# Two pads that move the weight tiles of a hybrid decoder layer to another place within 256 bytes

## The chip, the cores and the metric

The kernel runs on one core of one Trainium2 chip. The metric is the device time of one execution, in microseconds (us); the median of three runs is taken. Engines are named as in the profile: PE (the matrix engine, its matmuls), PEld (its loads of stationary weights, which overlap matmuls), DVE (vector), ACT (scalar), POOL and SP.

## The reference

One layer on 512 tokens of 1024 channels, in float32. Three sub-layers, each with an RMS norm, a scale and shift that come from a conditioning vector, and a gate on the residual:

```
h = modulate(rmsnorm(x, g1), sh1, sc1);  x = x + 0.5 * gt1 * ((silu(h @ w1_gate) * (h @ w1_up)) @ w1_down)
h = modulate(rmsnorm(x, gm), sh2, sc2);  x = x + gt2 * hybrid_mixer(h)
h = modulate(rmsnorm(x, g2), sh3, sc3);  x = x + 0.5 * gt3 * ((silu(h @ w2_gate) * (h @ w2_up)) @ w2_down)
return rmsnorm(x, g_final)
```

The SwiGLU width is 2816. The mixer has one input projection, a gated convolution of width 3 on 512 channels, attention of 8 heads with a compressed and two full branches, group norms and an output projection. Of all this the two SwiGLU layers and the two projections of the mixer are most of the arithmetic.

## The kernel before

**Products.** Every large product is made of three matmuls, to keep float32 precision: each operand is split into a high and a low part of type fp32r, and `mm3` (L280) issues high by high, high weights by the low part of the moving operand, and low weights by the high part. A matmul loads a stationary block of 128x128 (the weights: tiles `whi`, `wlo`) and streams a moving operand of 512 or 256 columns (the activations: `hhi`, `hlo` for the normed residual, `ghi`, `glo` for the gated hidden values). All of them come from line L278, so the profile tells them apart by tile names: `b<-hhi,whi` writes a PSUM bank from moving `hhi` and weights `whi`.

**Phases.** SwiGLU one, mixer, SwiGLU two. A phase begins with `first_products` or `first_group` (L576): six column blocks grow side by side, channel block by channel block, as the parts of h come. In the mixer and in SwiGLU two these are halves of 256 tokens. Then whole column blocks follow with 512 columns (`project` L545, `part` L609). The last two channel blocks of a SwiGLU (`main`, last loop) are again made in halves of 256 tokens.

**Weights.** Units of up to 1024 columns come from HBM into four tiles `raw` (L326), ACT copies the high part into one of four tiles `whi` (L366), DVE or POOL subtracts to get the low part in `wlo` (L355). A unit of 1024 columns holds eight blocks of 128 columns, 512 bytes apart in a partition. Some units at the end of a phase are needed twice and have memory of their own: in SwiGLU one two pairs `whik`, `wlok` (L585) from the phase's own pool, in the mixer two tiles `PT`.

**Order.** A list scheduler inside the kernel (`Plan`) gives each engine its instructions once, when the program is built. It knows costs of operations and nothing of addresses.

**Memory.** Tiles of the pool `const` lie one behind the other in each partition. Where a tile begins, in bytes and as the remainder by 256, follows from the sizes of those ahead of it. In this kernel:

| tiles | first begins at | remainder by 256 |
|---|---|---|
| raw0 to raw3 | 53184 | 192 |
| whi0 to whi3, then wlo0 to wlo3 | 69568 | 192 |
| hhi0 to hhi7, hlo0 to hlo7 | 102784 | 128 |
| ghi, glo (SwiGLU one, SwiGLU two) | 160128, 147840 | 128 |
| whik0, wlok0, whik1, wlok1 (SwiGLU one) | 209280 | 128 |
| V (values of the attention, stationary) | 139648 | 128 |
| PT0 to PT3, PT4 (turned probabilities) | 176896, 222368 | 0, 160 |

All sizes involved are multiples of 256, and so are the offsets of the blocks of 128 columns and of the halves of 256 tokens; the remainder holds for every block in these tiles.

Of the kernel before, what the change touches and what calls it, by code (L numbers as in the profile page):

```python
# [10 lines left out]
F32 = mybir.dt.float32  # L11
F32R = mybir.dt.float32r
# [7 lines left out]
P = 128  # L20
T = 512
D = 1024
DK = D // P
F = 2816
FK = F // P
FH = FK // 2
NB = T // P
HD = 64
# [12 lines left out]
# columns of the packed per-channel vectors  # L41
# [8 lines left out]
# columns of the packed constants  # L50
# [9 lines left out]
# slots of memory in turns  # L60
# [27 lines left out]
# the steps to a power of -0.5: (u + RS_P) u + RS_Q is next to u ** -0.5 / c for u about 1, and RS_K = 1 / (4 c c)  # L88
RS_P, RS_Q, RS_K = -3.333049194662436, 4.993328488220333, 1 / (4 * 0.3759002861170453 ** 2)
BATCHES = ((0,), (1,), (2, 3))  # L90
# ranks of the tasks: the lower goes first
# [33 lines left out]
class Slots:  # L125
    """Tokens for memory that is used over and over."""
# [4 lines left out]
    def spare(self, n):  # L131
        """A token, if n more stay idle."""
        return self, n


class Plan:
    """A list schedule of the core's work. Each task is a generator that asks for an engine and a time (or for
    one of several), for an event or for a token, and emits its instructions as the engine falls to it. The engines
    then run what they were given in that order."""

    # from engine (row) to engine (column)
# [105 lines left out]
def c_dma(n):  # L247
    """n: bytes of a partition."""
    return DMA, max(0.05, n * 0.356e-3)
# [6 lines left out]
def tile_hymba_layer(ctx: ExitStack, tc: tile.TileContext, xT, pos, cols_d, con_d, wa0, wa1, f1a, f1b, f1d,  # L256
# [23 lines left out]
    def mm3(o, w, x_, start, stop):  # L280
        """Both operands as (high, low) parts; low times low is below float32's last place."""
        mm(o, w[0], x_[0], start, False)
        mm(o, w[0], x_[1], False, False)
        mm(o, w[1], x_[0], False, stop)

# [41 lines left out]
    whi_of = [const.tile([P, UNIT], F32R, name=f"whi{i}") for i in range(N_W)]  # L327
    wlo_of = [const.tile([P, UNIT], F32R, name=f"wlo{i}") for i in range(N_W)]
# [4 lines left out]
    # the last units of a phase, needed twice, have memory of their own  # L333
# [50 lines left out]
    def rsqrt(v, y, u, alone=False):  # L384
        """y = (v / RS_K) ** -0.5 for normal v > 0: a guess from the exponent, a step of third order, one of second.
        alone: the vector engine takes nothing else in between."""
        guess = float(0x5f3759df - (2 << 23) - (1 << 31))
        yield SMALL
        nc.vector.tensor_scalar(y.bitcast(I32), v.bitcast(I32), -0.5, guess, op0=OP.mult, op1=OP.add)
        if alone:  # L390
            plan.limit[DVE] = R_NORM
        yield SMALL
        nc.vector.scalar_tensor_tensor(u, y, 16.0, y, op0=OP.mult, op1=OP.mult)  # L393
        yield SMALL
        nc.vector.tensor_mul(u, u, v)
        yield SMALL
        nc.vector.scalar_tensor_tensor(u, u, RS_P, u, op0=OP.add, op1=OP.mult)
        yield SMALL
        nc.vector.scalar_tensor_tensor(y, u, RS_Q, y, op0=OP.add, op1=OP.mult)
        yield SMALL  # L400
        nc.vector.scalar_tensor_tensor(u, y, 4.0 / RS_K, y, op0=OP.mult, op1=OP.mult)
        yield SMALL
        nc.vector.tensor_mul(u, u, v)
        yield SMALL
        nc.vector.scalar_tensor_tensor(y, u, 3.0, y, op0=OP.subtract, op1=OP.mult)
        if alone:
            plan.limit[DVE] = 1000

# [10 lines left out]
    class Norm:  # L419
        """1 / rms per token, from the channel blocks as they are ready: on every partition, or for the halves in  # L420
        columns with a token per partition."""
# [7 lines left out]
        def sums(self, i, o, s, start, stop):  # L429
            """Over the partitions of s, tokens on the partitions of the result."""  # L430
            ts = HALVES[i]
            nb = T // 2 // P
            for t in range(nb):
                mm(o[:, t:t + 1], s[:, ts.start + t * P:ts.start + (t + 1) * P], kv("one"), start and t == 0,
                   stop and t == nb - 1)
# [77 lines left out]
    def build_h(s, d, ts, rb, ready, used=lambda: None):  # L513
        """h, in parts: the normed residual, scaled and shifted."""
        n = ts.stop - ts.start
        q = yield scr
        t = scr_of[q][:, :n]
        yield c_stt(n)
        nc.vector.scalar_tensor_tensor(t, x[d][:, ts], am[:, s, d:d + 1], rb(), op0=OP.mult, op1=OP.mult)  # L519
        used()  # L520
        sh = mod[:, 3 * s, d:d + 1]
        yield c_act(n)
        nc.scalar.activation(hhi[d][:, ts], t, AF.Identity, bias=sh)  # L523
        yield c_stt(n)
        nc.vector.scalar_tensor_tensor(hlo[d][:, ts], t, sh, hhi[d][:, ts].bitcast(F32), op0=OP.add, op1=OP.subtract)  # L525
        give(scr, q)
        done(ready)
# [8 lines left out]
    def project(b):  # L536
        """A column block of the products with h, into bank b."""
# [7 lines left out]
    def start_builds(s, norm):  # L545
        """The parts of the next phase's h, as the norm allows."""
# [14 lines left out]
    def first_group(order, built, accs, end, n_cols=2 * GRP):  # L561
        """Some column blocks' products, channel block by channel block, as the parts of h come."""
# [150 lines left out]
    def ada_first(d):  # L713
        """Channel block d's shift and scale: summed over the blocks of c, then over the partitions."""
# [43 lines left out]
    def ada_first_pe(d):  # L758
        """The same by the tensor engine alone, four blocks of c side by side."""
# [51 lines left out]
    def warm():  # L811
        """Keeps the tensor engine at its full clock until the first products."""
# [57 lines left out]
    def ada_reduce(m, j):  # L870
        """Sums over the partitions: four rows of 256 channels, then turned to a channel per partition."""
# [30 lines left out]
    def rope_tables():  # L902
        """cos and sin of position x frequency, in steps; the angle is first taken to [-pi, pi]."""
# [58 lines left out]
    with ExitStack() as mixer:  # L962
# [52 lines left out]
        def rope(b, then, pool, scale=1.0):  # L1015
            """r * cos + swapped r * sin, then then(...). The queries are scaled, and negated: the scores' maxima are
            then the products' minima, as the exponents need them."""
# [51 lines left out]
        def keys(b):  # L1069
            """Per group: the high parts twice, for the queries' two parts; the low parts in place."""  # L1070
# [9 lines left out]
        def query(c):  # L1080
            """Per head: its high parts on the group's partitions, its low parts on the others."""
# [11 lines left out]
        def blocks(src, pn, i):  # L1093
            """The overlapping blocks of a compressed branch, with their position terms, in parts."""
# [40 lines left out]
        def compressed_keys(bs):  # L1135
            """From the two compressions' hidden sums (values, then keys) to their rows."""
# [57 lines left out]
        def compressed(c):  # L1194
            """Gated probabilities of the compressed branch of pair c: [2 x 32 keys, tokens]."""
# [36 lines left out]
            # rows without a valid key are all in the first block of tokens  # L1232
# [20 lines left out]
        # a pair's products with the values' low parts  # L1253
# [4 lines left out]
        def group_norm(y, gcol, n):  # L1258
            """y [P, T], two groups of 64 channels: normed in place."""
# [45 lines left out]
        def scores(c, b, s, n_, order):  # L1305
            """Probabilities of a head and branch, gated; then turned, in parts, for the products with the values."""
# [110 lines left out]
        def values(c, s):  # L1417
            """A head's sums over both branches, low parts of the values on the second 64 partitions."""
# [112 lines left out]
        def receive(f, b, pool, n):  # L1531
            """Starts what follows column block f of the input projection."""
# [150 lines left out]
        def keep():  # L1683
            """The turned probabilities' memory, for units once the attention is over."""
# [18 lines left out]
    with tc.tile_pool(name="g2", bufs=1) as gp:  # L1703
# [33 lines left out]
        def turn(g):  # L1737
            """Four channel blocks by 128 tokens."""
# [31 lines left out]
def _ffn_layout(wg, wu, wd):  # L1770
    g = wg.reshape(DK, P, FK, P)
    u = wu.reshape(DK, P, FK, P)
    gu = np.stack([g, u], axis=3)                      # k, p, f, 2, n
    first = gu[:, :, :GRP].reshape(DK, P, GRP * 2 * P)
    rest = gu[:, :, GRP:].transpose(2, 3, 1, 0, 4).reshape(FK - GRP, 2, P, DK * P)
    dn = wd.reshape(2, FH, P, DK, P)                   # half, k, p, d, n
# [5 lines left out]
def _layout(i):  # L1782
# [10 lines left out]
    def pose(p):  # L1793
        q = p.reshape(16, 2, HD).transpose(2, 1, 0).reshape(HD, 32)   # d, (parity, step)
        return np.concatenate([q, q])
# [41 lines left out]
    first = wa.reshape(DK, P, 9, DK, P)[:, :, :2]      # k, p, (shift, scale), d, n  # L1837
# [23 lines left out]
    wo = np.concatenate([wo[:512], wo[512:][perm]], axis=0).reshape(DK, P, DK, P)   # k, p, d, n  # L1861
# [31 lines left out]
```

## Time and profile before

| | |
|---|---|
| runs | 1083.23, 1082.0, 1084.75 us; median 1083.23 us |
| profiled execution, span from first to last instruction | 1081.2 us |
| what lies around the span, against the median | 2.0 us |
| PE busy | 1062.0 us, 98% |
| PEld busy | 860.6 us, 80% |
| DVE, ACT, POOL busy | 606.7, 409.9, 49.8 us |

The profile lists no time of the profiled execution beside its span, so the second and third line together stand for it. Matmuls are pipelined: the duration that a row gives one matmul overlaps the next one, so what a matmul costs the engine is read from start to start. A row `300.06 0.40 PE ...` of the view in order of time says when it began and how long it is shown; only the first number is used here.

### The profile page before, as it was taken

The numbers are of one execution on the slowest core, as the hardware profiler recorded it, in microseconds if no ns is written. First come the engines' busy times: TensorE is split into PE (matmuls) and PEld (weight loads), VectorE is DVE, ScalarE is ACT, GpSimd is POOL, SyncE is SP. The second block draws the span as 40 slices with busy tenths as digits, with TensorE's granted clock in tenths as the row PEclk, the third lists the DMA queues.
The fourth block names the chain that finished last, engine by engine and source line by source line (L and its number), as shares of the span: only waits on it lengthen the run. The fifth ranks groups of instructions, "written<-read, shape, count | busy, mean of one in ns | idle before, by whom it ended". The sixth has DMA issues, their size and how long they took to land.

```text
span 1081.2 us, 13889 instructions
## 1 busy us (share of the span) xinstructions
PE 1062.0 (98%) x5417; PEld 860.6 (80%) x5417; DVE 606.7 (56%) x1069; ACT 409.9 (38%) x713; POOL 49.8 (5%) x47
## 2 busy tenths in 40 slices
PE   8999999999999999999999999999999999999997
PEld 5777677788888889987777777998888888888887
DVE  4978888833333347499787786654333323333334
ACT  4552222212222233358756785334222122222321
POOL 0310000000000001012001010100000000000000
PEclk8999999999999999999999999999999999999998
DMA  9659989532222230443300003224333333322302
GB/s 333 243 191 326 315 322 327 176 96 85 92 98 98 98 103 16 131 125 122 127 25 28 13 14 96 92 83 132 94 89 91 98 98 98 94 86 93 98 20 78
DMA packets 40706, 133.60 MB, mean 124 GB/s; under 512 B 4704, under 2 KB 8032, under 8 KB 40000
## 3 DMA queue, kind: packets, MB, share of 16 engines
q1 hardware_dynamic: 40640, 132.71, 37.3%
q8 instruction: 42, 0.69, 0.3%
q14 instruction: 24, 0.20, 0.1%
HBM read 130.14 MB, written 2.10 MB: 122 GB/s over the span
## 4 chain that ended last, share of the span: by engine, by line
PE 88%; DVE 5%; DMA 4%; issue 1%; ACT 0%; SPq 0%; DVEq 0%; ACTq 0%
PE b L278 86%; DMA araw<-in_wa_dram 3%; PE b L1396 2%; DVE ada L865 1%; DVE afirst L736 1%; DVE wlo L355 1%; DMA x<-in_xT_dram 1%; DVE s L519 1%; DMA raw<-in_f1b_dram 0%; PE b L1291 0%; DVE afirst L733 0%; DVE v L393 0%; PE b L1241 0%; DVE afirst L728 0%; ACT hhi L523 0%
## 5 line engine op out<-in xcount | busy, mean ns | idle before, releaser
L278 PE MATMUL b<-hhi,whi 128*128 128x512 f32 (+1 forms) x1020 | 386.1, 379 | 0.0
L278 PE MATMUL b<-hlo,whi 128*128 128x512 f32 (+1 forms) x1020 | 379.0, 372 | 0.5 <-DVE hlo L525 0.4
L278 PE MATMUL b<-hhi,wlo 128*128 128x512 f32 (+1 forms) x1020 | 378.7, 371 | 0.0
L366 ACT ACTIVATE whi<-raw 128x1024 fp32r<-128x1024 f32 (+3 forms) x176 | 178.1, 1013 | 461.8 <-PE b L278 319.8
L355 DVE TENSOR_TENSOR wlo<-raw,whi 128x1024 fp32r<-128x1024 f32 (+3 forms) x162 | 191.2, 1180 | 218.4 <-ACT whi L366 213.0
L278 PEld LDWEIGHTS b<-hhi,whi 128*128 128x128 f32 x1020 | 192.3, 189 | 41.5 <-issue 6.7
L278 PEld LDWEIGHTS b<-hhi,wlo 128*128 128x128 f32 x1020 | 192.5, 189 | 36.6
L278 PEld LDWEIGHTS b<-hlo,whi 128*128 128x128 f32 x1020 | 192.7, 189 | 34.9 <-DVE hlo L525 1.2
L278 PE MATMUL b<-ghi,whi 128*128 128x512 f32 (+1 forms) x364 | 138.2, 380 | 0.0
L278 PE MATMUL b<-ghi,wlo 128*128 128x512 f32 (+1 forms) x364 | 137.4, 378 | 0.0
L278 PE MATMUL b<-glo,whi 128*128 128x512 f32 (+1 forms) x364 | 137.4, 378 | 0.0
L600 DVE TENSOR_TENSOR s<-sg,b 128x512 f32<-128x512 f32 x44 | 30.1, 686 | 106.6 <-PE b L278 105.8
L278 PEld LDWEIGHTS b<-ghi,whi 128*128 128x128 f32 x364 | 68.4, 188 | 14.7 <-issue 0.8
L278 PEld LDWEIGHTS b<-ghi,wlo 128*128 128x128 f32 x364 | 68.5, 188 | 14.0
L278 PEld LDWEIGHTS b<-glo,whi 128*128 128x128 f32 x364 | 68.5, 188 | 13.9
L865 DVE SCALAR_TENSOR_TENSOR ada<-araw,cact,ada 128x1024 f32<-128x1024 f32 x49 | 66.7, 1360 | 16.8 <-DMA araw<-in_wa_dram 16.1
L532 DVE SCALAR_TENSOR_TENSOR x<-b,mod,x 128x512 f32<-128x512 f32 (+1 forms) x30 | 19.1, 643 | 42.3 <-PE b L278 42.3
L450 ACT ACTIVATE s<-x 128x256 f32<-128x256 f32 (+1 forms) x41 | 19.4, 491 | 56.8 <-DVE x L532 53.7
L355 POOL TENSOR_TENSOR wlo<-raw,whi 128x768 fp32r<-128x768 f32 (+2 forms) x14 | 30.8, 2197 | 217.8 <-ACT whi L366 162.8
L605 ACT ACTIVATE ghi<-s 128x512 fp32r<-128x512 f32 x44 | 27.5, 631 | 15.7 <-DVE s L600 15.7
L523 ACT ACTIVATE hhi<-s,mod 128x256 fp32r<-128x256 f32 (+1 forms) x42 | 20.8, 533 | 31.5 <-DVE s L519 28.5
L1407 DVE TENSOR_TENSOR PT<-b,PT 128x384 fp32r<-128x384 f32 (+1 forms) x48 | 28.2, 598 | 5.0 <-ACT PT L1405 4.5
(238 smaller groups left out, 969.0 us busy)
## 6 DMA issues: line engine op xcount, KB each, us to landing
araw<-in_wa_dram SPq DMA_DIRECT2D x56, 512.0 KB
raw<-in_f1b_dram SPq DMA_DIRECT2D x38, 512.0 KB
raw<-in_f2b_dram SPq DMA_DIRECT2D x38, 512.0 KB
raw<-in_f1d_dram SPq DMA_DIRECT2D x22, 512.0 KB
raw<-in_f2d_dram SPq DMA_DIRECT2D x22, 512.0 KB
raw<-in_wib_dram SPq DMA_DIRECT2D x14, 512.0 KB
wfirst<-in_wa_dram SPq DMA_DIRECT2D x5, 1024.0 KB
raw<-in_wc_dram SPq DMA_DIRECT2D x8, 512.0 KB
```

The lines of the kernel that those rows point to most:

```text
L278: nc.tensor.matmul(o, lhsT, rhs, start=start, stop=stop)
L355: (nc.vector if e == DVE else nc.gpsimd).tensor_sub(wlo_of[j][:, :n], raw_of[i][:, :n], whi_of[j][:, :n].bitcast(F32))
L366: nc.scalar.activation(whi_of[j][:, :n], raw_of[raw_at[u]][:, :n], AF.Copy)
L450: nc.scalar.activation(o[:, ts], x[d][:, ts], AF.Square)
L519: nc.vector.scalar_tensor_tensor(t, x[d][:, ts], am[:, s, d:d + 1], rb(), op0=OP.mult, op1=OP.mult)
L523: nc.scalar.activation(hhi[d][:, ts], t, AF.Identity, bias=sh)
L532: nc.vector.scalar_tensor_tensor(x[d][:, ts], bank_of[b][:, ts], gate, x[d][:, ts], op0=OP.mult, op1=OP.add)
L600: nc.vector.tensor_mul(scr_of[q], sg_of[k], bank_of[bu])
L605: nc.scalar.activation(ghi[j], scr_of[q], AF.Copy)
L865: nc.vector.scalar_tensor_tensor(a, w, cact[:, k:k + 1], a, op0=OP.mult, op1=OP.add)
L1396: nc.tensor.transpose(pt[:, w:w + P], Pr[t][:, kb * P:(kb + 1) * P], ident)
L1407: nc.vector.tensor_sub(pl[:, :w], pt[:, :w], ph[:, :w].bitcast(F32))
```

## The change

Two pads of 192 and 64 bytes in each partition are put around the eight tiles `whi` and `wlo`, and these are made in turns (whi0, wlo0, whi1, ...) and no longer first the four `whi`. No instruction uses the pads. The tiles now begin at 69760 and every 4096 bytes after that, remainder 128; together the pads are 256 bytes, so every tile behind them keeps its remainder. What precedes them stays where it was, `raw` at 192 included. `whik`, `wlok` and `PT` keep their remainders too.

```
+    def lag(n, pool=const):
+        if n:
+            pool.tile([P, n // 4], F32, name=f"lag{next(lags)}")
+
+    lags = iter(range(100))
...
     raw_of = [const.tile([P, UNIT], F32, name=f"raw{i}") for i in range(N_RAW)]
-    whi_of = [const.tile([P, UNIT], F32R, name=f"whi{i}") for i in range(N_W)]
-    wlo_of = [const.tile([P, UNIT], F32R, name=f"wlo{i}") for i in range(N_W)]
+    whi_of, wlo_of = [], []
+    for i, n in enumerate((192, 0, 0, 0)):
+        lag(n)
+        whi_of.append(const.tile([P, UNIT], F32R, name=f"whi{i}"))
+        wlo_of.append(const.tile([P, UNIT], F32R, name=f"wlo{i}"))
+    lag(64)
```

The rest of the diff takes comments away. Each engine has the same instructions with the same tiles and waits in the same order as before; addresses alone differ.

## Rows read from the trace of the kernel before

**Rows 1.** The page: span, engines (busy, share, instructions), granted clock in 40 slices.
```profile
span 1081.2 us, 13889 instructions
PE 1062.0 (98%) x5417; PEld 860.6 (80%) x5417; DVE 606.7 (56%) x1069; ACT 409.9 (38%) x713; POOL 49.8 (5%) x47
PEclk8999999999999999999999999999999999999998
```

**Rows 2.** Stretches: us, busy (x instructions) by engine, granted clock, DMA share, GB/s.
```profile
50.00:131.00 81.00, 76.61 (x346) 59.31 (x345) 67.08 (x74) 28.25 (x45) 9.11 (x5) 0.99 0.75 261
131.00:200.00 69.00, 69.00 (x317) 53.47 (x315) 58.12 (x60) 17.88 (x22) 0.00 (x0) 0.98 0.91 322
200.00:415.00 215.00, 215.00 (x981) 175.69 (x978) 83.53 (x109) 57.07 (x71) 0.00 (x0) 1.00 0.28 92
```

**Rows 3.** The chain that ended last, by line, in 50:131 and then 131:1081.2.
```profile
by line: DMA araw<-in_wa_dram 41.7%; DVE ada L865 15.8%; issue 8.7%; PE b L278 6.8%; DVE wlo L355 6.1%; DMA raw<-in_f1b_dram 5.8%; DVE afirst L736 4.5%; DVE ada L862 1.8%; DVE s L600 1.5%; DVE glo L607 1.5%; ACT whi L366 1.3%; DVE afirst L7
...
by line: PE b L278 95.5%; PE b L1396 1.9%; PE b L1291 0.4%; PE b L1241 0.2%; PE b L1746 0.2%; DVE v L389 0.2%; PE b L492 0.1%; PE b L884 0.1%; DVE wlo L355 0.1%; issue 0.1%; PE b L1272 0.1%; DVE o L1754 0.1%; DVE z L1294 0.1%; DVEq L1887 0.
```

**Rows 4.** Groups by form from 131 us on, 512 columns: xcount | busy, mean | idle.
```profile
L278 PE MATMUL b<-hhi,whi 128*128 128x512 f32 x690 | 278.6, 404 | 0.0
L278 PE MATMUL b<-hhi,wlo 128*128 128x512 f32 x691 | 273.6, 396 | 0.0
...
L278 PE MATMUL b<-ghi,whi 128*128 128x512 f32 x308 | 122.2, 397 | 0.0
```

**Rows 5.** PE in order of time (start us, us shown), 512 columns, SwiGLU one.
```profile
299.83 0.39 PE L278 MATMUL b<-hhi,whi 128*128 128x512 f32 x1
...
320.83 0.39 PE L278 MATMUL b<-hhi,whi 128*128 128x512 f32 x1
```

**Rows 6.** Groups by form from 131 us on, 256 columns.
```profile
L278 PE MATMUL b<-hhi,whi 128*128 128x256 f32 x192 | 53.6, 279 | 0.0
...
L278 PE MATMUL b<-ghi,whi 128*128 128x256 f32 x56 | 16.0, 285 | 0.0
```

**Rows 7.** PE in order of time, first group of the mixer.
```profile
425.18 0.28 PE L278 MATMUL b<-hlo,whi 128*128 128x256 f32 x1
425.30 0.28 PE L278 MATMUL b<-hhi,wlo 128*128 128x256 f32 x1
...
440.05 0.28 PE L278 MATMUL b<-hhi,whi 128*128 128x256 f32 x1
...
450.25 0.28 PE L278 MATMUL b<-hhi,whi 128*128 128x256 f32 x1
```

**Rows 8.** PE in order of time, last halves of SwiGLU one.
```profile
403.05 0.28 PE L278 MATMUL b<-ghi,whi 128*128 128x256 f32 x1
...
404.07 0.28 PE L278 MATMUL b<-ghi,whik 128*128 128x256 f32 x1
...
407.67 0.28 PE L278 MATMUL b<-ghi,whik 128*128 128x256 f32 x1
```

**Rows 9.** PE in order of time, last halves of SwiGLU two.
```profile
1061.15 0.28 PE L278 MATMUL b<-glo,whi 128*128 128x256 f32 x1
...
1063.27 0.28 PE L278 MATMUL b<-glo,whi 128*128 128x256 f32 x1
```

**Rows 10.** PE in order of time, mixer: matmuls ahead of one with weights V.
```profile
553.40 0.40 PE L278 MATMUL b<-hhi,wlo 128*128 128x512 f32 x1
553.63 0.62 PE L278 MATMUL b<-PT,V 128*128 128x512 f32 x2
...
595.31 0.40 PE L278 MATMUL b<-hhi,wlo 128*128 128x512 f32 x1
595.54 0.62 PE L278 MATMUL b<-PT,V 128*128 128x512 f32 x2
596.00 0.27 PE L1396 MATMUL b<-con,stab 128*128 128x128 f32 x1
```

**Rows 11.** Groups by form on DVE: the low parts of the weights.
```profile
L355 DVE TENSOR_TENSOR wlo<-raw,whi 128x1024 fp32r<-128x1024 f32 x136 | 166.3, 1224 | 188.9 <-ACT whi L366 183.5 <-PE b L278 0.8
...
L355 DVE TENSOR_TENSOR wlok<-raw,whik 128x1024 fp32r<-128x1024 f32 x2 | 2.4, 1217 | 0.0
```

## The prediction

> **What bounds the kernel now.** I read the page first: PE is busy 98% of a span of 1081.2 us, and its granted clock is at nine tenths or more of the upper level (2.4 GHz) but for the first and the last slice [rows 1]. So only what changes the pace of PE can change the time much. The stretches and the chain then say from where on. Between 50 and 131 us the chain runs over the transfers of the conditioning weights (41.7%) and DVE's sums, and PE is only 6.8% of it [rows 3]; PE idles 4.4 of 81 us there [rows 2]. From 131 us on PE's products of L278 are 95.5% of the chain [rows 3], and from 131 to 415 us PE has no idle time at all [rows 2]. From there to the end each ns that a matmul takes, start to start, is a ns of the kernel; the 2.0 us between the span and the median of 1083.23 us are not touched, so the change is added to the median.
>
> The question is then what one matmul costs from start to start, and whether that depends on where its weights lie. Five places in order of time tell it. Matmuls with 512 columns: from 299.83 to 320.83 us there are 30 groups of three, 90 matmuls in 21.00 us, 233.3 ns each [rows 5]. With 256 columns and the same `whi` tiles: 90 matmuls from 440.05 to 450.25 us, 113.3 ns each [rows 7]; nine from 403.05 to 404.07 us, also 113.3 ns [rows 8]; but 18 from 1061.15 to 1063.27 us, 117.8 ns each [rows 9]. So at one and the same place (weights at 192, activations at 128) two paces are seen. With weights in `whik` and `wlok`, which lie at 128 as the activations do, 30 matmuls from 404.07 to 407.67 us take 120.0 ns each [rows 8]. They are the same matmuls of the same loop, one after the other, with the weights in another tile. That is the only steady stretch of before with both operands at the same place, and it is the slowest of the three.
>
> **The change part by part.** It adds and removes no instruction and moves none, on no engine and no queue. What remains are four things that addresses can do.
>
> *256 columns.* From 131 us on `hhi,whi` has 192 of them, `hlo,whi` and `hhi,wlo` as many, and the three kinds with `ghi`, `glo` 56 each [rows 6]: 576 in the first groups of the mixer and of SwiGLU two, 168 in the tails of the two SwiGLU. I give all of them the 120.0 ns of `whik` afterwards. The 576 went at 113.3 ns, but for some at the beginning of a group, which go 0.12 us apart already [rows 7]; I take 40 as such. (576 - 40) x 6.7 ns = 3.6 us. The 168 are in part at 113.3 and in part at 117.8 ns, so between 2.2 and 6.7 ns each; with the middle, 4.5 ns, 0.75 us. Sum: +4.3 us, all on the path. Bounds: if the 120.0 ns came from something other than the place, 0; if all 744 paid 6.7 ns, +5.0 us.
>
> *512 columns.* The large term: three kinds with 690, 690 and 691 and three with 308 each, 2995 matmuls on the path [rows 4]; 1 ns on each is 3.0 us. Nowhere before do 512 columns stream steadily with weights at the same place, so I bound it. The unit is the 6.7 ns between the fast pace and that of `whik`. Up: a step once for each matmul, +20.1 us; twice, if it goes with columns, +40. Down: at the 0.443 ns a column of the fast 256s a 512 would take 226.7 ns, again 6.7 ns, -20.1 us. Nearest are four places in the mixer where one 512 streams `hhi` at 128 while the weights V, also at 128, are loaded for the next. It goes on to the next start in 0.23 us (two of the four are shown) [rows 10], and the two matmuls behind it take 0.46 us together. That is the usual 233 ns, neither 227 nor 240. Against it: with `whik` too the first step showed nothing, 404.07 is 0.11 us behind its predecessor, and only from the second on it was 0.12. Still the second matmul at V is not late either. I take 0 for the 512s.
>
> A reason why it may be 0: with 256 columns the next weights have barely time to arrive, with 512 there is twice that. A load that is somewhat late then shows in the first case and is covered in the second. The cover is 233.3 - 113.3 = 120 ns, far more than a step of 6.7 ns.
>
> *Before 131 us.* Some 340 matmuls with 512 and 72 with 256 columns lie there. A loss of a few ns on each is hidden by the transfers that the chain waits for [rows 3]. A gain is hidden as well.
>
> *ACT and DVE*, which write these tiles. DVE makes `wlok` (at 128) in 1217 ns and `wlo` (at 192) in 1224 ns [rows 11], both from `raw` at 192. The difference is nothing, and after 131 us neither is on the chain. Cost 0; covered by PE.
>
> Sum: 1083.2 + 4.3 = 1087.5 us.
>
> **The rivals.**
>
> *Slower in the 512s too.* Mechanism: the weight load and the moving stream want the same part of the memory at the same time, and the stream stands still for it, whatever its length. For it: the only steady stretch at the same place is the slow one [rows 8], and the 512s run at 0.456 ns a column, above the 0.443 of the fast 256s [rows 5, 7], so something does hold them up. Against it: the places at V [rows 10]. One step for each, 20.1 + 4.3: 1107.6 us; a third of a step, 1094 us.
>
> *Faster.* The 512s are held up now, by 6.7 ns against the pace per column of the fast 256s. If the place of 192 against 128 is what holds them up, and 128 against 128 frees them, each gains 6.7 ns: -20.1 us, and 1067.4 us if the 256s lose their 4.3; 1062 if they also gain, the slow ones the 4.5 ns to the fast pace (0.8 us). It decides from the second 512 on, in every block. Between 131 and 200 us the DMA engines are at 0.91 [rows 2] and might give back 2 us of it. For it: 256s at the very same place have two paces, so the place alone is not the pace, and what is slow for one length can be fast for another. Against it: `whik`, and the unchanged starts at V.
>
> The Trainium skill, page "TensorE: Matmul & The Clock Gate", section "Back-to-back issue gap", gives about 216 ns for 512 columns in a row. The trace does not agree here, with 233.3 ns [rows 5]. By that figure an estimate of the most that any change of place could free is 17 ns for each of the 2995, some 52 us; no row shows such a pace, and I give it no chance of its own.
>
> *No effect.* The 120.0 ns of `whik` may belong to something else: those tiles lie far up in the partition, and their pace began after another kind of block. Then nothing changes: 1083.2 us. For it: the two paces at one place show that the history of the stream counts. Against it: the change from 113.3 to 120.0 comes within two matmuls of the change of tile.
>
> The Trainium skill, page "SBUF — State Buffer", section "SBUF: two separate sides", speaks for this rival: PE has its own read side, and the engines contend only where DVE and GpSimd share a port. By it no place is slower than another, and the time would stay at 1083.2 us. The trace does not settle it: the two paces at one place [rows 7, 9] need some other cause in any case, but the change of pace at `whik` [rows 8] the rule would leave unexplained.
>
> **How the numbers follow.** Forecast (512s unmoved, 256s at 120 ns): 1087.5 us, chance 0.40; the spread of the term, 1083.2 to 1090 us. Slower in the 512s: 0.17 (of it 0.05 for a third of a step). Faster: 0.28. No effect: 0.15. To hold 0.8 the range must reach to the faster case, 1062 us, and at the other end to 1098 us, above the third of a step; the full step (0.12) and a gain beyond 1062 stay out. A measurement of this kernel can tell about 0.3%, 3.2 us, from no change. The forecast is just above that; I count 0.08 of its 0.40 as within. Faster 0.28; within 0.15 + 0.08 = 0.23; slower 0.32 + 0.17 = 0.49. Both signs are possible, so the likeliest case's own range is 1083 to 1090 us.
>
> **What would show it.** In the profile after, in order of time: three 512s take 0.70 us now. If they still do, the large term is 0 as taken; 0.72 is the slower rival, 0.68 the faster one. In the first group of the mixer, three 256s take 0.34 us now; 0.36 confirms the small term, 0.34 means no effect. The tail of SwiGLU one should lose its change of pace at `whik`: 0.36 before and behind it. From 200 to 415 us the count of matmuls (981 now) tells the same in one row. I am wrong if the 512s move at all, since 1 ns there weighs almost as much as the whole small term.

## The result

The changed kernel took 1070.63 us (median of five runs, 1068.77 to 1075.31) against 1083.19 us for the kernel before, 0.9889 of it with a 95% interval from 0.9868 to 0.9910: faster by 1.1%, 12.6 us. A second series gave 1070.87 us, 0.9890 (0.9872 to 0.9908). The forecast was 1087.5 us, so the time moved the other way; it is nearest to the rival called "Faster", at 1067.4 us.

The page of the changed kernel, span, PE and granted clock in 40 slices, as in [rows 1]:

```profile
span 1073.5 us, 13889 instructions
PE 1048.8 (98%) x5417; PEld 865.9 (81%) x5417; DVE 607.3 (57%) x1069; ACT 409.2 (38%) x713; POOL 50.1 (5%) x47
PEclk8899999999999999999999899999999999999998
```

PE is busy 98% as before, with the same 5417 instructions, but for 13.2 us less. Now four stretches, as in [rows 2]; the first two are those of [rows 2], the others are new (columns: us, busy (x instructions) of PE, PEld, DVE, ACT, POOL, granted clock, DMA share, GB/s):

```profile
131.00:200.00 69.00, 65.62 (x299) 51.91 (x297) 56.46 (x57) 17.10 (x22) 0.00 (x0) 0.98 0.89 310
200.00:415.00 215.00, 214.13 (x1020) 179.89 (x1021) 88.97 (x122) 59.57 (x77) 0.15 (x1) 1.00 0.27 93
600.00:605.00 5.00, 5.00 (x32) 3.87 (x32) 3.63 (x12) 3.83 (x12) 0.00 (x0) 1.00 0.01 3
607.00:613.00 6.00, 6.00 (x23) 3.36 (x21) 1.84 (x10) 1.86 (x9) 0.00 (x0) 0.50 0.00 0
```

Between 200 and 415 us 1020 matmuls stand where 981 stood. Between 131 and 200 us PE now idles 3.4 us, where it did not idle at all. The last stretch is a disturbance of this one execution, which is the slowest of its five: for some 7 us the granted clock was 0.50, the lower of the two levels (1.2 of 2.4 GHz), though PE was busy all the time there and in the stretch ahead of it. It costs 2.9 us (the rest of the mixer, matmul by matmul against before, loses 1.7 us in this execution and gains 1.2 in the second series) and is absent in the second series, whose span is 1069.3 us; accounts by stage below use that one.

PE in order of time (start us, us shown), with 512 columns as in [rows 5], then the tail of SwiGLU one as in [rows 8], then the first group of the mixer as in [rows 7]; line 285 is what line 278 was:

```profile
299.11 0.39 PE L285 MATMUL b<-hhi,whi 128*128 128x512 f32 x1
...
319.51 0.39 PE L285 MATMUL b<-hhi,whi 128*128 128x512 f32 x1
...
399.63 0.28 PE L285 MATMUL b<-glo,whi 128*128 128x256 f32 x1
399.75 0.28 PE L285 MATMUL b<-ghi,wlo 128*128 128x256 f32 x1
399.87 0.28 PE L285 MATMUL b<-ghi,whik 128*128 128x256 f32 x1
399.99 0.28 PE L285 MATMUL b<-glo,whik 128*128 128x256 f32 x1
...
436.75 0.28 PE L285 MATMUL b<-hhi,whi 128*128 128x256 f32 x1
...
447.55 0.28 PE L285 MATMUL b<-hhi,whi 128*128 128x256 f32 x1
```

Between the first two rows lie 90 matmuls in 20.40 us, 226.7 ns each: 6.7 ns less than before. Between the last two lie 90 in 10.80 us, 120.0 ns each: 6.7 ns more. At `whik` nothing changes any more.

### The profile page after: what moved, and what is told of

Read it like the earlier page. It is cut to its first block, busy times and chain, and to the rows that moved or that the text cites. A ratio compares the mean times of both kernels' runs of the same rounds, so it can differ in the third digit from the quotient of the medians.

```text
span 1073.5 us, 13889 instructions
## 1 busy us (share of the span) xinstructions
PE 1048.8 (98%) x5417; PEld 865.9 (81%) x5417; DVE 607.3 (57%) x1069; ACT 409.2 (38%) x713; POOL 50.1 (5%) x47
## 4 chain that ended last, share of the span: by engine, by line
PE 80%; DVE 9%; DMA 7%; issue 2%; ACT 1%; SPq 0%; DVEq 0%; ACTq 0%
PE b L285 77%; DMA araw<-in_wa_dram 6%; DVE ada L876 3%; PE b L1407 2%; DVE wlo L366 1%; DVE s L530 0%; ACT whi L377 0%; DVE afirst L747 0%; DMA raw<-in_f1b_dram 0%; DMA x<-in_xT_dram 0%; DVE s L611 0%; DVE glo L618 0%; PE b L1302 0%; DVE s L1050 0%; DVE swp L1053 0%
## 5 line engine op out<-in xcount | busy, mean ns | idle before, releaser
L1416 ACT ACTIVATE PT<-b 128x384 fp32r<-128x384 f32 (+1 forms) x48 | 24.5, 524 | 17.9 <-PE b L1407 17.3
```

Source lines behind the costliest of these rows:

```text
L1416: nc.scalar.activation(ph[:, :w], pt[:, :w], AF.Copy)
```

## Where the time went

Each matmul of the kernel before was paired with the same one in the second series of the changed kernel. The second column counts the 512-column matmuls with weights in `whi` and `wlo` of the stage, the third multiplies them by -6.7 ns, the last is by how much the lead of the changed kernel grew (-) or shrank (+).

| stage, us of before | 512 columns | at -6.7 ns each | measured |
|---|---|---|---|
| 0 to 131.0 | 342 | hidden | -2.4 |
| 131.0 to 200.1 | 276 | -1.8 | +2.5 |
| 200.1 to 415.1, SwiGLU one and its tail | 864 | -5.8 | -5.6 |
| 415.1 to 460.1, first group of the mixer | 0 | 0 | +1.7 |
| 460.1 to 690.1, rest of the mixer | 480 | -3.2 | -1.2 |
| 690.1 to 740.2, first group of SwiGLU two | 27 | -0.2 | +1.6 |
| 740.2 to 1045.1, SwiGLU two | 1307 | -8.7 | -8.7 |
| 1045.1 to 1073.3, its tail | 40 | -0.3 | +0.2 |

The sum of the last column is -11.9 us, the difference of the two spans (1081.2 and 1069.3). From 200 us on the column repeats: two more kernels with these relative places (the place alone and both at 192, below), paired in the same way, come within 0.2 us of it in every stage. The first two rows do not repeat: over the kernels below the difference to before at 200 us lies between -2.4 and +2.0 us, the latter in one with the old pace.

Two stages give less than the pace says. Up to 200 us everything gained is handed back in this pair. PE waits between 131 and 200 us, in the second series and in the order alone, a kernel of the next section that has the pace of before (us in total, times, longest; of before this view has no row there):

```profile
PE b L285 <- DVE ada L876: 3.2, 2, 2.4
...
PE b L285 <- DVE ada L876: 3.1, 1, 3.1
```

PE is sooner at the point where it needs the sums of the conditioning vector, and those wait for transfers that come no sooner. The last of these sums, in before (two in one row) and in the second series, DVE in order of time:

```profile
196.75 2.60 DVE L865 SCALAR_TENSOR_TENSOR ada<-araw,cact,ada 128x1024 f32<-128x1024 f32 x2 [0.31 <-DMA araw<-in_wa_dram]
...
198.23 1.28 DVE L876 SCALAR_TENSOR_TENSOR ada<-araw,cact,ada 128x1024 f32<-128x1024 f32 x1 [0.20 <-DMA araw<-in_wa_dram]
```

They end at 199.4 and 199.5 us. As the order alone shows, PE can wait there at the old pace too; that before had no idle time in this stretch belongs to its one traced execution. In the mixer the products are cut into short runs. PE in order of time, second series:

```profile
549.26 0.40 PE L285 MATMUL b<-hhi,wlo 128*128 128x512 f32 x1
549.49 0.62 PE L285 MATMUL b<-PT,V 128*128 128x512 f32 x2
549.96 0.27 PE L1407 MATMUL b<-con,P 128*128 128x128 f32 x1
...
560.83 0.40 PE L285 MATMUL b<-hhi,whi 128*128 128x512 f32 x1
...
562.23 0.34 PE L285 MATMUL b<-ks,q 128*128 128x384 f32 x1
```

From 560.83 to 562.23 us six matmuls of 512 columns take 1.40 us, 233 ns each, with both operands at 128. Paired by the length of the run, a matmul takes 1.5 ns more than before in the 22 runs of three, 1.3 ns less in the 18 runs of six, and 6.2 ns less in the two runs of 93: most runs here end before the pace is there. The 512s gain 1.7 us in this stage in place of 3.2, and some 0.4 us is lost at the matmuls between them. And the place at V, 0.23 us and then 0.47 us for two, is what it was in [rows 10], though everything around it has changed.

## The experiments

**Which part of the edit.** Three kernels: the place without the new order, the order without the new place, and the other operand moved in place of the weights.

```
# the place alone
+    lag(192)
     whi_of = [const.tile([P, UNIT], F32R, name=f"whi{i}") for i in range(N_W)]
     wlo_of = [const.tile([P, UNIT], F32R, name=f"wlo{i}") for i in range(N_W)]
+    lag(64)
# the order alone: whi0, wlo0, whi1, ... as in the change, but
-    for i, n in enumerate((192, 0, 0, 0)):
+    for i, n in enumerate((0, 0, 0, 0)):
...
-    lag(64)
+    lag(256)
# both at 192: as the order alone, but lag(64) behind the weights
```

> The pads alone: first the four whi, then the four wlo, as before, but at remainder 128. If the place against h and g is the cause, the 512-column matmuls of the steady stretches go 226.7 ns from start to start and the 256-column ones 120.0 ns, and the time is that of the changed kernel, 1069 to 1072 us. If the making in turns is the cause, 233.3 ns and 113.3 to 117.8 ns stay, and 1082 to 1085 us.

> The making in turns alone: whi0, wlo0, whi1, ... at remainder 192, with all 256 bytes of pad behind them. If the place is the cause: 233.3 ns for 512 columns, 113.3 to 117.8 ns for 256, and 1082 to 1085 us, as before. If the distance between a whi and its wlo (4096 bytes and no longer 16384) is the cause: 226.7 ns, 120.0 ns and 1069 to 1072 us.

> Weights at 192 as before, but a pad of 64 bytes behind them moves h, g, V and the kept weights to 192 as well. If it counts that both operands have the same remainder: 226.7 ns for 512 columns, 120.0 ns for 256, and 1069 to 1072 us. If the weights' own place counts, 128 being the good one: 233.3 ns and 113.3 to 117.8 ns, and 1082 to 1085 us. If 192 is bad for both operands, slower than 1085 us.

The stretch from 250 to 350 us, all of it 512 columns, in the three kernels in this order:

```profile
250.00:350.00 100.00, 100.00 (x443) 82.82 (x442) 34.90 (x37) 28.99 (x38) 0.00 (x0) 1.00 0.27 95
```

```profile
250.00:350.00 100.00, 100.00 (x430) 80.62 (x429) 33.67 (x36) 28.42 (x36) 0.00 (x0) 1.00 0.27 93
```

```profile
250.00:350.00 100.00, 100.00 (x443) 82.84 (x442) 34.27 (x37) 28.34 (x36) 0.00 (x0) 1.00 0.27 96
```

100 us by 443 matmuls is 226 ns each, by 430 it is 233 ns. The times: place alone 1071.88 us, ratio 0.9895 (0.9880 to 0.9910); order alone 1084.11 us, 1.0009 (0.9991 to 1.0027); both at 192 1070.76 us, 0.9885 (0.9868 to 0.9901). So the making in turns does nothing, and 128 is not a good place in itself: what counts is where the weights lie relative to the moving operand.

**A scan in one trace.** The four pairs of tiles are used in turns, eight blocks each time. With a different remainder for each pair, one trace shows four places.

```
-    for i, n in enumerate((192, 0, 0, 0)):
+    for i, n in enumerate((64, 64, 64, 64)):
...
-    lag(64)
```

> Made in turns, the four pairs whi, wlo at remainders 0, 64, 128 and 192, one pair each, so that one trace shows four places against h and g at 128. If the place relative to the moving operand sets the pace: 226.7 ns (512) and 120.0 ns (256) with the pair at 128, 233.3 ns and 113.3 to 117.8 ns with the pair at 192; for 0 and 64 the theory gives no number, and the old paces or the new ones are both open. If a stream keeps the pace that it fell into, whatever the place, one pace will run through all four pairs. Time between 1069 and 1090 us.

PE in order of time in this kernel, the first matmul of each visit. In the first five rows, with 512 columns, the pairs at 128, 192, 0, 64 and again 128 begin. In the rest, with 256 columns, visits begin and end with the pair at remainder 64 (64 bytes behind h), with the one at 128, and with the one at 64 again:

```profile
291.46 0.39 PE L285 MATMUL b<-hhi,whi 128*128 128x512 f32 x1
...
296.91 0.40 PE L285 MATMUL b<-hhi,whi 128*128 128x512 f32 x1
...
302.51 0.39 PE L285 MATMUL b<-hhi,whi 128*128 128x512 f32 x1
...
308.08 0.39 PE L285 MATMUL b<-hhi,whi 128*128 128x512 f32 x1
...
313.59 0.39 PE L285 MATMUL b<-hhi,whi 128*128 128x512 f32 x1
...
422.75 0.28 PE L285 MATMUL b<-hhi,whi 128*128 128x256 f32 x1
...
424.87 0.28 PE L285 MATMUL b<-hhi,whi 128*128 128x256 f32 x1
...
429.14 0.28 PE L285 MATMUL b<-hhi,whi 128*128 128x256 f32 x1
...
431.30 0.28 PE L285 MATMUL b<-hhi,whi 128*128 128x256 f32 x1
...
435.49 0.28 PE L285 MATMUL b<-hhi,whi 128*128 128x256 f32 x1
...
437.53 0.28 PE L285 MATMUL b<-hhi,whi 128*128 128x256 f32 x1
```

A visit with 512 columns has 24 matmuls: 5.45 us at 128 (227.1 ns each), 5.60 at 192 (233.3), 5.57 at 0 (232.1), 5.51 at 64 (229.6). The pace changes within a few matmuls of the pair, and comes back in every round. At 128 the first starts, from 291.46 us on, are 228, 232, 231, 227, 227, 226 ns apart: three matmuls pass until the pace is there. With 256 columns 18 matmuls take 2.12 us (117.8 ns), 2.16 (120.0) and 2.04 (113.3): at 128 always 120.0 when steady, at 64 two paces. The time of this kernel, 1076.87 us in its one run, is between the two kernels'.

Three more kernels of this kind: places by 32 bytes, whi and wlo of a pair at different places, and steps of 8 and 16 bytes.

```
# by 32 bytes
+    for i, n in enumerate((32, 64, 64, 64)):
...
+    lag(32)
# pulled apart: tiles in the order of their places
+    for n, names in ((0, ("wlo0", "whi1")), (64, ("wlo3",)), (64, ("wlo2",)), (64, ("whi0", "whi2", "whi3", "wlo1"))):
+        lag(n)
+        for name in names:
+            slot[name] = const.tile([P, UNIT], F32R, name=name)
...
# by 16 bytes: whi and wlo in one tile, OFF columns of 4 bytes into it
+    pair, OFF = [], (4, 4, 2, 4)
+    for n in (160, 0, 224, 0):
+        lag(n)
+        pair.append(const.tile([P, 2 * UNIT + 8], F32R, name=f"whi{len(pair)}"))
+    whi_of = [p[:, o:o + UNIT] for p, o in zip(pair, OFF)]
...
```

> The four pairs at remainders 224, 32, 96 and 160, which is 96 ahead, 160 ahead, 32 behind and 32 ahead of h and g at 128. The theory of the relative place says that each pair has its own pace, kept from visit to visit, between 226.7 and 233.3 ns for 512 columns and between 113.3 and 120 ns for 256; it gives no order among the four. If only whole steps of 64 bytes count, 96 and 160 will go as 64 or 128 do in the scan by 64 (229 to 230 and 226.7 ns). Against the theory: one pace in all four. Time 1069 to 1087 us.

> The pairs are pulled apart: whi at 128 with wlo at 192, whi at 192 with wlo at 128, whi at 128 with wlo at 64, whi at 128 with wlo at 0. If each load counts for itself, a pair with one of its two tiles at 128 lies between 226.7 and 233.3 ns (two of three loads are whi: about 229 ns for whi at 128 with wlo at 192, about 231 ns the other way round). If one badly placed load holds the whole round, both pairs of 128 and 192 go 233.3 ns. If only whi counts, 226.7 ns wherever whi is at 128.

> Each pair is one tile, and its blocks begin 16, 16, 8 and 16 bytes into it, so that the four pairs lie 16 bytes behind, 16, 8 and 48 bytes ahead of h and g. If nearness to the same place counts gradually, the pair 8 bytes off is close to 226.7 ns with 512 columns and the one 48 bytes off close to 233.3 ns. If only the exact place counts, all four go 231 to 234 ns. If one of them is better than the same place, below 226.7 ns. Time 1069 to 1087 us.

PE in order of time, pulled apart: the first matmul of the pairs (whi, wlo) at (192, 128), (128, 64), (128, 0), (128, 192), and the end of the last:

```profile
287.73 0.39 PE L285 MATMUL b<-hhi,whi 128*128 128x512 f32 x1
...
293.27 0.40 PE L285 MATMUL b<-hhi,whi 128*128 128x512 f32 x1
...
298.83 0.39 PE L285 MATMUL b<-hhi,whi 128*128 128x512 f32 x1
...
304.38 0.39 PE L285 MATMUL b<-hhi,whi 128*128 128x512 f32 x1
...
309.92 0.39 PE L285 MATMUL b<-hhi,whi 128*128 128x512 f32 x1
```

24 matmuls take 5.54, 5.56, 5.55 and 5.54 us, 230.8 to 231.7 ns each. That is between 226.7 and 233.3 for all four: neither does one badly placed tile hold the whole round, nor does whi alone count. But it is not the simple sum either, which asked for about 229 ns with only wlo off and 231 with only whi off; 230.8 was measured with either.

PE in order of time, steps of 16 bytes: the second matmul of the pairs 8, 48, -16 and 16 bytes ahead of h and g, and again the first of them:

```profile
291.23 0.39 PE L285 MATMUL b<-hlo,whi 128*128 128x512 f32 x1
...
296.77 0.40 PE L285 MATMUL b<-hlo,whi 128*128 128x512 f32 x1
...
302.38 0.39 PE L285 MATMUL b<-hlo,whi 128*128 128x512 f32 x1
...
307.87 0.39 PE L285 MATMUL b<-hlo,whi 128*128 128x512 f32 x1
...
313.46 0.39 PE L285 MATMUL b<-hlo,whi 128*128 128x512 f32 x1
```

5.54, 5.61, 5.49 and 5.59 us. By 32 bytes all four pairs took 5.60 or 5.61 us, which is close to the one pace for all that had been named as speaking against the theory; the other two scans, where the pairs differ, decide for it, and these four places are all bad. The times, one run each: by 32 bytes 1087.61 us, pulled apart 1080.40, by 16 bytes 1078.17. From the three scans, the mean distance of starts from the seventh to the 22nd matmul of the visits (465 to 512 distances for 512 columns, 100 to 181 for 256), by how far the weights lie ahead of h and g modulo 256:

| bytes ahead | -96 | -64 | -32 | -16 | 0 | 8 | 16 | 32 | 48 | 64 | 96 | 128 |
|---|---|---|---|---|---|---|---|---|---|---|---|---|
| 512 columns, ns | 233.3 | 229.0 | 233.3 | 228.3 | 226.8 | 230.6 | 232.8 | 233.4 | 233.3 | 233.3 | 234.3 | 232.1 |
| 256 columns, ns | 119.8 | 116.8 | 116.8 | 118.4 | 119.9 | 115.8 | 118.4 | 118.4 | 117.9 | 115.7 | 118.5 | 118.9 |

For 512 columns the same place is the best of the twelve. It is not a matter of the exact byte: 16 behind costs 1.5 ns, 8 ahead 3.8, and by 16 ahead nearly all is lost. The means for 256 columns mix the paces of a stream: at 64 and -64 the single streams go 113.3 or 117.8 ns.

That the remainder by 256 is the right measure is shown in part only. Taken by 512 bytes, the weights lie 64 ahead of h in the kernel before and 320 ahead in the order alone, and both go 233.3 ns; the columns -16, 16 and 96 of the table lie at 240, 272 and 352. But wherever 226.7 ns were measured, the two remainders agree by 512 as well (weights from 69760, h from 103040 in the changed kernel), and no run has the operands exactly 256 bytes apart.

**Is it the place that makes whik slow?** The kernel before, with one pad ahead of the kept weights (and 256 bytes of pad behind the eight weight tiles, as in the order alone).

```
+        lag(64, gp)
         for k in range(KEEP[s]):
             whi_of.append(gp.tile([P, UNIT], F32R, name=f"whik{k}"))
```

> The kernel before (weights at 192, h and g at 128) with one pad of 64 bytes ahead of the kept weights of SwiGLU one, which brings them from 128 to 192. If the place is what made them slow, their 30 matmuls in a row with 256 columns go 113.3 or 117.8 ns, and the change of pace at whik is gone. If they are slow for another reason (they lie far up, or what ran before them), 120.0 ns stays. Time as before within 1 us.

PE in order of time in this kernel, kept weights:

```profile
404.22 0.28 PE L285 MATMUL b<-glo,whik 128*128 128x256 f32 x1
...
407.62 0.28 PE L285 MATMUL b<-glo,whik 128*128 128x256 f32 x1
...
407.85 0.50 PE L285 MATMUL b<-con,ssum 128*128 128x1 f32 x4
...
408.64 0.28 PE L285 MATMUL b<-ghi,whik 128*128 128x256 f32 x1
...
409.94 0.28 PE L285 MATMUL b<-ghi,wlok 128*128 128x256 f32 x1
```

30 matmuls in 3.40 us, 113.3 ns each, where [rows 8] had 120.0: it was the place. Behind the four small matmuls of 407.85 us the same tiles go 11 in 1.30 us, 118 ns each. So the two paces at 64 bytes apart are two states of a stream, and an interruption can change one into the other. The time is 1083.83 us, in its one run, as before. In its trace the first group of the mixer, at the same remainders by 256 as before, also ran in the 117.8 ns state where before had 113.3, which costs 1.1 us: what decides between the two states no run shows.

**The better of both.** If 512 columns want the same place and 256 columns want 64 bytes between, the weights of the first groups can simply begin 16 columns further into their tile; these units have 768 of 1024 columns, so there is room.

```
+    halves = {*range(n_ffn, n_ffn + DK), *range(n_mix, n_mix + DK)}
+
+    def at(u):
+        return 16 if u in halves else 0
...
-        i = w_at[u]
-        return whi_of[i][:, j * n:(j + 1) * n], wlo_of[i][:, j * n:(j + 1) * n]
+        i, a = w_at[u], at(u) + j * n
+        return whi_of[i][:, a:a + n], wlo_of[i][:, a:a + n]
```

ACT and the subtraction write at the same offset. The second of the two kernels also has the pad ahead of `whik`; the changed kernel ran beside it.

> The changed kernel, but the weights of the first groups of the mixer and of SwiGLU two (256 columns) begin 64 bytes further into the same tiles, at remainder 192; all else stays at 128. If the pace follows the place of each block of weights: 512 columns stay at 226.7 ns, the 576 matmuls with 256 columns of these groups go back from 120.0 to 113.3 ns, and the time is 3 to 4 us below that of the changed kernel, 1066 to 1068 us. If the pace of 256 columns was lost for another reason, 1069 to 1072 us.

> The changed kernel once more, on the same chip as the next one: 1069 to 1072 us; 512 columns at 226.7 ns, 256 columns at 120.0 ns.

> The changed kernel with the 256-column weights of both first groups at 192, as in the run before, and also the kept weights of SwiGLU one (whik, wlok) moved by 64 bytes to 192. By the pace of each place: 2 to 4 us below the changed kernel run beside it, of which the kept weights give at most 0.4 us (some 60 matmuls by 6.7 ns); 1066 to 1068.5 us. If the difference of the halves was chance, the two kernels agree within 1 us.

The two first groups, mixer and SwiGLU two, in the changed kernel and in the last one:

```profile
430.00:450.00 20.00, 20.00 (x169) 20.00 (x168) 5.70 (x8) 5.74 (x8) 0.00 (x0) 1.00 0.35 122
705.00:725.00 20.00, 20.00 (x169) 20.00 (x168) 8.55 (x14) 6.20 (x10) 0.00 (x0) 1.00 0.34 106
```

```profile
430.00:450.00 20.00, 20.00 (x176) 20.00 (x175) 7.41 (x10) 7.42 (x10) 0.00 (x0) 1.00 0.43 143
705.00:725.00 20.00, 20.00 (x179) 20.00 (x178) 7.32 (x10) 6.40 (x9) 0.00 (x0) 1.00 0.41 132
```

The first of the two better kernels took 1068.06 us, 0.9864 of before (0.9841 to 0.9887). The 113.3 ns that were expected of both its first groups came in that of SwiGLU two alone; that of the mixer stayed in the 117.8 ns state throughout. The second took 1067.28 us, 0.9861 (0.9837 to 0.9885), beside 1070.87 us of the changed kernel. The intervals against before overlap. But the two traces, paired, show where the 3.6 us between the spans (1069.3 and 1065.7) come from: matmul by matmul the lead grows by 0.2 us in the tail of SwiGLU one, by 1.7 us in the first group of the mixer and by 1.8 us in that of SwiGLU two, and by nothing after 740 us.

## Why the prediction was wrong, step by step

*What bounds the kernel.* Right: PE from its starts, and each ns of a 512-column matmul counts almost in full in the two long stretches (-5.6 and -8.7 us). Wrong by a stage was the point from which it counts. PE had no idle time from 131 us on, which I read as bound by PE; but the order alone idles 3.1 us there at the old pace, a PE that is 6.7 ns faster only reaches the transfers sooner, and the path begins at 200 us. The note on the DMA share in the rival "Faster" had named that 2 us.

*256 columns.* Right in place, sign and size: 120.0 ns everywhere that a stream is steady, +1.7 and +1.6 us in the first groups, the latter net of 0.2 us that 512s give back. That is +3.5 us for a forecast of 3.6; the two tails, by what their stages fall short of the pace of the 512s, lose some 0.7 us for a forecast of 0.75. The kept weights with their pad show that the reason given, the place, was the reason.

*512 columns: the step that failed.* I took 0 for a term that was -6.7 ns each, a lower bound of my own. In the time it came to some -16 us: the 12.6 us gained and the 3.5 us or more that the 256s cost. The measured time lies between my 1062 and 1098 us only because that range had been stretched to a rival; the forecast's own spread began at 1083.2. The 0 rested on the four places at V. The changed kernel shows that these places can tell nothing: the 0.23 and 0.47 us at V stand there unchanged beside streams at 226.7 ns. One start behind a change of place is too early; the scan needs three matmuls until the pace is there. I had seen that at `whik`, where the first step showed nothing either, and set it aside for the second matmul at V, which is as little.

The second prop, that a late load is covered with 512 columns by 120 ns of spare time, fell too. The load has time to spare, and yet the place of the weights moves the pace by as much as with 256 columns, 6.7 ns, in the other direction. The loads between 250 and 350 us, of before and of the second series (count | busy, mean ns of one | idle before):

```profile
L278 PEld LDWEIGHTS b<-hhi,whi 128*128 128x128 f32 x144 | 27.1, 188 | 6.5
...
L285 PEld LDWEIGHTS b<-hhi,whi 128*128 128x128 f32 x148 | 27.8, 188 | 5.8
```

They take 188 ns in both, less than either pace, so by these records the spare time is about 40 ns and a late load is not what sets the pace. The Trainium skill, page "SBUF — State Buffer", section "SBUF: two separate sides", has PE wait on nobody on the engines' side of the memory. That is said of one engine and another and names no addresses; that by it no place is slower than another was read into it. The runs show what it does not speak of: with addresses alone changed, 233.3 ns became 226.7 and 113.3 became 120.0. And the 216 ns that the prediction quotes from the Trainium skill, page "TensorE: Matmul & The Clock Gate", section "Back-to-back issue gap", is called there the gap of a single matmul, with a lower figure for streams with weight loads; the fastest steady 512s of any run here take 226.7 ns.

*The rivals.* "Faster" had the mechanism, the unit and the point of decision right, with 0.28 for a chance. Against its 1067.4 us the median is 3.2 us higher. The table names what is missing: 1.8 us between 131 and 200 us, and 2.0 us in the mixer, where most runs of 512s are too short to fall into the pace. "Slower in the 512s" carried the finding at 256 columns over to 512; the slowest of the twelve places gives 234.3 ns, far from the 240.0 of a step. "No effect" fell with the kept weights. The order of the chances was wrong for one reason: the fast 256s show what a column can cost, 0.443 ns, and I gave that less weight than a row that was too short.

What stays open: why the same place is best for one length and worst for the other, and what in the memory or in PE's sequence makes steps of 6.7 ns. No run here looks inside.

## What to carry to other kernels

Where many matmuls with 512 columns follow each other with a new stationary tile each, as in this fp32r kernel, put the stationary and the moving tiles at the same remainder by 512 bytes (256 was not separated from it), and those with 256 columns 64 bytes apart, which gave 113.3 or 117.8 ns for 120.0; it costs a pad. Try places with several pads in one kernel and read one trace, start to start, from the fourth or fifth matmul of a stream on. A gain of pace that is earned before a transfer lands is given back there, even where the engine shows no idle time yet.

## What was not expected of the hardware

At the same place and at 64 bytes ahead the steady paces are 226.7 and 233.3 ns with 512 columns, 120.0 and 113.3 ns with 256, each pair 6.7 ns apart, 16 cycles of 2.4 GHz at a granted clock of 1.00; at other places the means lie between and, at 96 ahead, beyond. The 233.3 is itself a mean: single starts are 231 and 236 ns apart in turns, where those of the 226.7 are all 226 or 227. At 64 bytes apart a stream of 256 columns has two states, 113.3 and 117.8 ns; four small matmuls in between were enough to change it (407.85 us above). And in one execution the granted clock fell to 0.50 for about 7 us (607 to 613 us above) while PE had no idle time at all; why is not known.
